# Two decoder layers on one core: the first norm's factor applied behind the GLA products

## The chip, the cores and the metric

The kernel runs on one core of a Trainium2 chip. The metric is the device time of one execution in microseconds (us), as the median of several runs. A core has TensorE (PE in the profile; its weight loads are PEld), VectorE (DVE), ScalarE (ACT), GpSimd (POOL) and SyncE (SP), each with a program of its own, and 16 DMA engines that serve the queues of SP, ACT and POOL.

## The reference, cut to what matters

A prompt of 1024 tokens and eight sample tokens go through two layers of width 1024. Layer 0 has a gated linear attention (GLA, four heads), layer 1 a sliding-window softmax attention; each is followed by a feed-forward layer, and every sub-layer is wrapped in two norms:

```python
def rms_norm(x, g):
    y = xf * lax.rsqrt(jnp.mean(xf * xf, axis=-1, keepdims=True) + NORM_EPS)
    return (y * g.astype(jnp.float32)).astype(x.dtype)
...
h = x @ w_in                      # x is rms_norm(input, norm_mix_pre[0]); 3088 columns
q, k, v, r, z = jnp.split(h, ...) # 512, 512, 1024, 1024, 16
log_a = log_sigmoid(z @ w_gate2 + b_gate) / GLA_TAU
o, s_new = gla_recurrence(q, k, v, log_a, s0)
o = rms_norm(o, g_head) * silu(r)
...
hp = hp + rms_norm(mp, norm_mix_post[layer])
```

The norm in front of the GLA multiplies each feature by a gain and each token by one factor 1 / sqrt(mean(x^2) + eps). A product with `w_in` is linear, so a token's factor can be applied to its input or to each of its results.

## The kernel before

The tokens are worked on in two groups: A is prompt blocks 0 to 3 and the eight samples (520 tokens, in chunks of 256 and 264), B is prompt blocks 4 to 7 (512 tokens, one chunk). Activations have features on partitions, as tiles of 128 features by the tokens of a group, eight tiles for 1024 features.

Each product with a weight matrix is made of column tiles of 128 columns. Weights and activations are split into a high and a low part (`xh`, `xl`, `wh`, `wl`), and for each of eight feature tiles three products are added up: high by high (L217), low by high (L219), high by low (L221), 24 for one column tile and one chunk. `prep` fetches a column tile in two halves on SP's queue (three staging buffers `wst`), casts the high part on ScalarE (L204) and subtracts on VectorE (L205). A job is one column tile; its weights are prepared one job ahead. Results lie in three PSUM buffers (`ps_lin`); transposes and small products use five others (`aux`).

Work other than the jobs is background: generators in one queue, advanced by `tick` according to the us of products emitted since. The tile framework then orders each engine's instructions by readiness and program order; `keep_in_program_order` puts an instruction behind the one traced before it on its engine.

The first phase, group A: `load_x` fetches blocks of 128 tokens by 1024 features, tokens on partitions, on SP's queue. For each block `norm` squares and sums (ScalarE, L438), forms the factor in small steps (L441 to L446) and multiplies the block by factor and gain (VectorE, L449; the gain was fetched broadcast to 128 partitions). `turn` transposes the block on TensorE (L459) and splits it (L289, L290). Behind the third to fifth block come the weights of the gate's input z (`prep_z`) and of the first two column tiles of r. Then, chunk by chunk, z (L247), r0 and r1 are multiplied, and from r2 (t = 2) on the jobs run: six more tiles of r, then for each head q, k and two tiles of v. `gla_gate` turns z into decay tiles `eq` and `ek` for a head, one head ahead; `ev_q` and `ev_k` (L585, L589) multiply q and k by them on the way out of PSUM. `gla_inner` is the background work of a head: transposes, states (`Sp`, cleared by GpSimd at L650), sample states stored from GpSimd's queue (L710), norm. B's `load_x` is the first background task, with B's blocks brought in one by one into one buffer.

Later, after the output projections, `norms` adds the residual and normalises for the feed-forward layer. For the first sub-layer the residual is the input itself (`from_input`): for each of eight feature tiles it is fetched again on ACT's queue, turned on TensorE (L364; for A the samples too, L371) and added on VectorE (L366, L372). For later sub-layers (`from_scratch`) it is read from a scratch tensor `xs` in device memory that already has features on partitions, and added without TensorE. `need(nA)` forces A's norm to be complete ahead of its feed-forward layer.

Of the kernel before, what the change touches and what calls it, by code (L numbers as in the profile page):

```python
# [31 lines left out]
# tiles in a hidden block; buffers  # L32
# [6 lines left out]
# jobs of a feed-forward layer ahead of the projections put into it, and after its attention  # L39
# [4 lines left out]
# how thinly the background work is spread: factors for each norm, then the samples' and the prompt's attention  # L44
# [12 lines left out]
# and steps, in us of matrix products  # L57
# [11 lines left out]
def tile_hybrid_gla_swa_decoder(  # L69
# [10 lines left out]
    # two groups of tokens, features on partitions: A = prompt blocks 0..3 and the samples, B = blocks 4..7  # L80
# [37 lines left out]
    def halved(t, n, name):  # L118
        """-0.5 t, for the factor -2 that rstd_gen leaves"""
        o = const.tile([P, n], F32, name=name)  # L120
        nc.vector.tensor_scalar_mul(o, t, -0.5)
        return o

# [5 lines left out]
    def load_params():  # L129
# [11 lines left out]
        nc.vector.tensor_scalar_mul(bq8, bqkv_t[:, 0:8], 0.125)  # L141

# [21 lines left out]
    def after(jobs, gen, scale=1.0):  # L164
        """the jobs, and a task that is added when the last of them has been emitted"""
# [25 lines left out]
    def prep(w, row0, kt, col0, m, dst=None):  # L191
        parts = []
        for hf in range(kt // 4):
            st = wpool.tile([P, 4, P], F32, tag="wst", name="wst", bufs=WS)
            nc.sync.dma_start(
                out=st[:, :, :m],
                in_=w[row0 + hf * 512 : row0 + hf * 512 + 512, col0 : col0 + m].rearrange(
                    "(k p) m -> p k m", p=P))
# [1215 lines left out]
```

## Time and profile before

| | |
|---|---|
| runs before | 2284.96, 2286.06, 2286.59 us; median 2286.06 us |
| profiled execution: span | 2282.3 us; the page gives no other time for it |
| what lies around the span | 2286.06 - 2282.3 = 3.8 us, the median against the span |
| TensorE busy | 2255.3 us, 99% |
| VectorE, ScalarE, GpSimd busy | 1463.2, 1230.0 and 81.7 us (64%, 54%, 4%) |

A busy share counts an engine as busy from the start of an instruction to its modelled end; products overlap in the pipeline, so the distance between starts is the better measure of what one costs. An idle time is put down to what ended it last.

### The profile page before, as it was taken

The numbers are of one execution on the slowest core, as the hardware profiler recorded it, in microseconds if no ns is written. First come the engines' busy times: TensorE is split into PE (matmuls) and PEld (weight loads), VectorE is DVE, ScalarE is ACT, GpSimd is POOL, SyncE is SP. The second block draws the span as 40 slices with busy tenths as digits, with TensorE's granted clock in tenths as the row PEclk, the third lists the DMA queues.
The fourth block names the chain that finished last, engine by engine and source line by source line (L and its number), as shares of the span: only waits on it lengthen the run. The fifth ranks groups of instructions, "written<-read, shape, count | busy, mean of one in ns | idle before, by whom it ended". The sixth has DMA issues, their size and how long they took to land.

```text
span 2282.3 us, 39657 instructions
## 1 busy us (share of the span) xinstructions
PE 2255.3 (99%) x14764; PEld 2053.8 (90%) x14764; DVE 1463.2 (64%) x3186; ACT 1230.0 (54%) x2614; POOL 81.7 (4%) x121
## 2 busy tenths in 40 slices
PE   7999999999999999999999999999999999999998
PEld 6998889989999998998888989989999898888887
DVE  6587665676644457566887477658888478444445
ACT  6655544465434446545766456537766456434435
POOL 3010000100000000120000000020000000000000
PEclk9999999999999999999999999999999999999999
DMA  6443322445333335333222354432222353533332
GB/s 169 128 132 92 105 78 77 126 138 155 93 93 93 90 92 172 97 110 93 79 86 77 103 157 131 131 111 77 75 75 78 93 163 110 171 105 97 93 97 83
DMA packets 413634, 246.75 MB, mean 108 GB/s; under 512 B 17817, under 2 KB 400889, under 8 KB 412641
## 3 DMA queue, kind: packets, MB, share of 16 engines
q1 hardware_dynamic: 385344, 196.85, 30.0%
q10 hardware_dynamic: 24000, 25.58, 3.8%
q0 software_dynamic: 4096, 21.79, 2.8%
q8 instruction: 116, 1.90, 0.4%
q14 instruction: 78, 0.63, 0.1%
HBM read 220.67 MB, written 24.25 MB: 107 GB/s over the span
## 4 chain that ended last, share of the span: by engine, by line
PE 95%; DVE 2%; DMA 1%; ACT 1%; issue 0%; POOL 0%; ACTq 0%; DVEq 0%; POOLq 0%
PE psl L219 29%; PE psl L217 29%; PE psl L221 29%; PE psc L978 1%; PE ppt L1007 1%; PE po L1018 1%; PE po L1019 1%; PE pP L657 1%; PE pO L684 0%; PE pO L682 0%; PE pxi L364 0%; PE pvt L629 0%; PE patt L633 0%; DMA cm<-const_cmask_dram 0%; DVE nxn L334 0%
## 5 line engine op out<-in xcount | busy, mean ns | idle before, releaser
L217 PE MATMUL psl<-xh,wh 128*128 128x512 f32 (+2 forms) x2784 | 890.8, 320 | 0.7 <-ACT sr L511 0.3
L221 PE MATMUL psl<-xh,wl 128*128 128x512 f32 (+2 forms) x2784 | 886.0, 318 | 1.8 <-DVE xss L445 1.7
L219 PE MATMUL psl<-xl,wh 128*128 128x512 f32 (+2 forms) x2784 | 886.6, 319 | 0.0
L204 ACT CAST wh<-wst 128x512 fp32r<-128x512 f32 x712 | 440.9, 620 | 717.1 <-PE psl L219 629.7
L205 DVE TENSOR_TENSOR wl<-wst,wh 128x512 fp32r<-128x512 f32 x712 | 497.5, 700 | 347.2 <-ACT wh L204 310.9
L221 PEld LDWEIGHTS psl<-xh,wl 128*128 128x128 f32 x2784 | 523.3, 188 | 39.1 <-DVE wl L205 2.4
L217 PEld LDWEIGHTS psl<-xh,wh 128*128 128x128 f32 x2784 | 524.1, 188 | 37.6 <-ACT sr L511 0.6
L219 PEld LDWEIGHTS psl<-xl,wh 128*128 128x128 f32 x2784 | 523.9, 188 | 35.8
L221 PE MATMUL psl<-hh,wl 128*128 128x256 f32 (+2 forms) x1536 | 487.3, 317 | 0.0
L217 PE MATMUL psl<-hh,wh 128*128 128x256 f32 (+1 forms) x1504 | 479.6, 319 | 0.0
L219 PE MATMUL psl<-hl,wh 128*128 128x256 f32 (+1 forms) x1504 | 479.2, 319 | 0.0
L221 PEld LDWEIGHTS psl<-hh,wl 128*128 128x128 f32 x1536 | 288.9, 188 | 20.5
L217 PEld LDWEIGHTS psl<-hh,wh 128*128 128x128 f32 x1504 | 283.0, 188 | 20.8 <-ACT hh L289 0.3
L219 PEld LDWEIGHTS psl<-hl,wh 128*128 128x128 f32 x1504 | 282.7, 188 | 20.7 <-DVE hl L290 0.3
L793 DVE TENSOR_TENSOR yf<-yf,psl 128x256 f32<-128x256 f32 (+1 forms) x344 | 172.4, 502 | 151.7 <-PE psl L221 150.2
L290 DVE TENSOR_TENSOR hl<-rl,hh 128x256 fp32r<-128x256 f32 (+1 forms) x192 | 98.8, 515 | 144.5 <-ACT hh L289 144.4
L780 ACT ACTIVATE rl<-psl 128x256 f32<-128x256 f32 (+1 forms) x192 | 87.1, 454 | 63.1 <-PE psl L221 57.5
L781 ACT ACTIVATE rl<-rl 128x256 f32<-128x256 f32 (+1 forms) x192 | 94.5, 492 | 4.6
L289 ACT CAST hh<-rl 128x256 fp32r<-128x256 f32 (+1 forms) x192 | 92.3, 481 | 4.7
L305 DVE TENSOR_TENSOR nacc<-nacc,nsq 128x520 f32<-128x520 f32 (+1 forms) x99 | 68.6, 693 | 17.3 <-ACT nsq L304 15.0
L992 ACT ACTIVATE pb<-pb,mx 128x256 f32<-128x256 f32 (+1 forms) x128 | 62.2, 487 | 5.7 <-DVE mx L990 4.7
L984 DVE CUSTOM_DVE_ANT_0 pb<-psc,smask 128x256 f32<-128x256 f32 (+1 forms) x128 | 47.8, 401 | 1.2 <-PE psc L978 1.1
(332 smaller groups left out, 2011.8 us busy)
## 6 DMA issues: line engine op xcount, KB each, us to landing
wst<-in_ffn_w_up_dram SPq DMA_DIRECT2D x256, 256.0 KB
wst<-in_ffn_w_down_dram SPq DMA_DIRECT2D x256, 256.0 KB
wst<-in_gla_w_in_dram SPq DMA_DIRECT2D x96, 256.0 KB
wst<-in_swa_w_qkv_dram SPq DMA_DIRECT2D x48, 256.0 KB
wst<-in_gla_w_out_dram SPq DMA_DIRECT2D x32, 256.0 KB
wst<-in_swa_w_out_dram SPq DMA_DIRECT2D x32, 256.0 KB
nx<-xs ACTq DMA_DIRECT2D x24, 260.0 KB
xs<-y POOLq DMA_DIRECT2D x2, 2080.0 KB, 7.9
```

Source lines behind the costliest of these rows:

```text
L204: nc.scalar.copy(out=wh[:, :, :m], in_=st[:, :, :m])
L205: nc.vector.tensor_tensor(out=wl[:, :, :m], in0=st[:, :, :m], in1=r(wh[:, :, :m]), op=ALU.subtract)
L217: nc.tensor.matmul(o, lhsT=wh[:, k % 4, :m], rhs=xh[:, k, c0:c0 + n], start=(k == 0), stop=False)
L219: nc.tensor.matmul(o, lhsT=wh[:, k % 4, :m], rhs=xl[:, k, c0:c0 + n], start=False, stop=False)
L221: nc.tensor.matmul(o, lhsT=wl[:, k % 4, :m], rhs=xh[:, k, c0:c0 + n], start=False, stop=(k == kt - 1))
L289: nc.scalar.copy(out=h, in_=src)
L290: nc.vector.tensor_tensor(out=l, in0=src, in1=r(h), op=ALU.subtract)
L305: nc.vector.tensor_tensor(out=acc, in0=acc, in1=sq, op=ALU.add)
L780: nc.scalar.activation(out=rl, in_=ps, func=AF.Relu)
L781: nc.scalar.activation(out=rl, in_=rl, func=AF.Square)
L793: nc.vector.tensor_tensor(out=o, in0=o, in1=ps, op=ALU.add)
L992: nc.scalar.activation(out=pb[:, i, k0:], in_=pb[:, i, k0:], func=AF.Exp, bias=mx[:, i:i + 1], accum_out=st[:, 2 + i:3 + i])
```

## The change

Group A's input is no longer normalised before it is turned. `load_a` works on two blocks at a time: it transposes the raw blocks, two feature tiles at a time (`turn_pair`: four transposes into one PSUM tile), multiplies by the gain only (now one column `g1` with features on partitions, made by transposing a small tile `g8`), and splits. The squares and the factors are taken beside it. The factors reach all partitions as `rsA` by a product of ones with a diagonal tile `dg`. The raw transposed input is copied from PSUM and written to `xs` from ACT's queue, eight transfers of 256 KB, so A's first residual is read by `from_scratch`; `from_input` stays for B.

The factor then goes to the results: z and r are multiplied by `rsA` as they leave PSUM, on VectorE (r left by ScalarE before); `eq` and `ek` of each head are multiplied by `rsA` on GpSimd; v's turned tiles are scaled on ScalarE, in four instructions in place of two, and the samples' v on VectorE.

The order of the first phase changes too: blocks 0 and 1, both halves of r0's weights, r1's weights (into a free half of scratch), z's weights (one transfer in place of two), blocks 2 and 3 and the samples are all fetched on SP without waiting for a buffer. The weights of r0 are prepared between the turned pairs; r1's low parts are subtracted on GpSimd. Chunk 0 is multiplied as r0, r1, z, with the second pair's turning put in between, then chunk 1. `load_gate` moves behind these products, and its two instructions, the small `halved` ones and one other are pinned in program order. B's input is loaded two blocks at a time by `load_b` with more steps: scaled on ScalarE, turned by `turn_pair`. A's raw blocks now lie in the buffer of B's low parts. The rest of the diff removes comments.

```diff
+    g8 = const.tile([KT, P], F32, name="g8")
+    nc.scalar.dma_start(out=g8, in_=n_mix_pre[0].rearrange("(k p) -> k p", p=P))
+    g1 = const.tile([P, KT], F32, name="g1")
+    pg = aux([P, KT], "pg")
+    nc.tensor.transpose(pg, g8, ident[:KT, :KT])
+    nc.vector.tensor_copy(out=g1, in_=pg)
...
+    def prep(w, row0, kt, col0, m, dst=None, pin=False, sts=None, between=(), eng=None):
...
+                st = sts[hf]
             if dst is None:
                 wh = wpool.tile([P, 4, P], F32R, tag="wh", name="wh", bufs=WB)
...
-            nc.scalar.copy(out=wh[:, :, :m], in_=st[:, :, :m])
-            nc.vector.tensor_tensor(out=wl[:, :, :m], in0=st[:, :, :m], in1=r(wh[:, :, :m]),
-                                    op=ALU.subtract)
+            pinned(nc.scalar.copy(out=wh[:, :, :m], in_=st[:, :, :m]), pin)
+            pinned((eng or nc.vector).tensor_tensor(out=wl[:, :, :m], in0=st[:, :, :m], in1=r(wh[:, :, :m]),
+                                                    op=ALU.subtract), pin)
             parts.append((wh, wl))
+            if hf < len(between):
+                between[hf]()
...
-            if g.ns:
-                xm = npool.tile([NS, P], F32, tag="xsm", name="xsm", bufs=1)
-                nc.scalar.dma_start(out=xm, in_=x_sample[:, 0, k * P:(k + 1) * P])
-                ps = aux([P, NS], "pxs")
-                nc.tensor.transpose(ps, xm, ident[:NS, :NS])
-                nc.vector.tensor_tensor(out=y[:, k, TB:TB + NS], in0=y[:, k, TB:TB + NS], in1=ps, op=ALU.add)
...
-    gbc, xtk = scr[:, 0:D], scr[:, 3 * D:4 * D]
+    rsA, xsm, zt = scr[:, 0:NMAX], scr[:, NMAX:NMAX + 128], scr[:, NMAX + 128:NMAX + 392]
+    xtk = [scr[:, D:2 * D], scr[:, 3 * D:4 * D]]
+    A.rt = const.tile([P, 5], F32, name="rtA")
...
+    def turn_pair(k, tiles, h, l, c0, pin):
+        pt = aux([P, 2, 256], "xT")
+        for i in range(2):
+            for q in range(2):
+                nc.tensor.transpose(pt[:, q, i * P:(i + 1) * P], tiles[i][:, (k + q) * P:(k + q + 1) * P], ident)
+        for q in range(2):
+            hk, lk, g_ = h[:, k + q, c0:c0 + 256], l[:, k + q, c0:c0 + 256], g1[:, k + q:k + q + 1]
+            pinned(nc.scalar.activation(out=hk, in_=pt[:, q, :], func=AF.Copy, scale=g_), pin)
+            pinned(nc.vector.scalar_tensor_tensor(out=lk, in0=pt[:, q, :], scalar=g_, in1=r(hk),
+                                                  op0=ALU.mult, op1=ALU.subtract), pin)
+        return pt
...
+    def load_a(h, l, pair, tiles):
+        c0 = pair * 256
+        ns = NS if pair == 1 else 0
+        n = 3 if ns else 2
+        ss = gp.tile([P, 9], F32, tag="xss", name="xss", bufs=4)
...
+        prs = aux([P, 512], "prs")
+        squares(ss, 0, tiles[0])
+        raw = []
+        for k in range(0, KT, 2):
+            raw.append(turn_pair(k, tiles, h, l, c0, True))
+            yield
+        pinned(squares(ss, 1, tiles[1]))
+        if ns:
+            pinned(squares(ss, 2, tiles[2], NS))
+        y = A.rt[:, 2 * pair:2 * pair + n]
+        factors(ss, n, y)
...
+        N = 256 + ns
+        dg = nt(N, "dg")
+        for i in range(2):
+            nc.vector.tensor_scalar_mul(dg[:, i * P:(i + 1) * P], ident, y[:, i:i + 1])
+        nc.tensor.matmul(prs[:, :256], lhsT=ones, rhs=dg[:, :256], start=True, stop=True)
...
+        nc.scalar.copy(out=rsA[:, c0:c0 + N], in_=prs[:, :N])
+        for k, pt in zip(range(0, KT, 2), raw):
+            t = gp.tile([P, NMAX], F32, tag="qd" if k < 4 else "ki", name="xr", bufs=2)
+            t = t[:, :512].rearrange("p (k t) -> p k t", t=256)
+            pinned(nc.scalar.copy(out=t, in_=pt))
+            nc.scalar.dma_start(out=xs[0][:, k:k + 2, c0:c0 + 256], in_=t)
...
+    def load_b():
+        h, l = new_xn(B)
+        xB.append((h, l))
+        for pair in range(2):
+            ss = gp.tile([P, 9], F32, tag="xss", name="xss", bufs=4)
+            for i in range(2):
+                fetch(B, 2 * pair + i, xtk[i])
+            yield YD
+            for i in range(2):
+                squares(ss, i, xtk[i])
+            y = const.tile([P, 2], F32, name=f"rtB{pair}")
+            factors(ss, 2, y)
+            yield YD
+            for i in range(2):
+                nc.scalar.activation(out=xtk[i], in_=xtk[i], func=AF.Copy, scale=y[:, i:i + 1])
+                yield YN
+            for k in range(0, KT, 2):
+                turn_pair(k, xtk, h, l, pair * 256, False)
+                yield YN
...
         def ev_z(ps, c0, n):
             z = g.z3[:, c0:c0 + n]
+            if g.rs is not None:
+                t = zt[:2 * RANK, :n]
+                nc.vector.tensor_tensor(out=t, in0=ps, in1=g.rs[:2 * RANK, c0:c0 + n], op=ALU.mult)
+                ps = t
...
-            return lambda ps, c0, n: nc.scalar.copy(out=g.sr[:, t, c0:c0 + n], in_=ps)
+            def f(ps, c0, n):
+                o = g.sr[:, t, c0:c0 + n]
+                if g.rs is None:
+                    nc.scalar.copy(out=o, in_=ps)
+                else:
+                    pinned(nc.vector.tensor_tensor(out=o, in0=ps, in1=g.rs[:, c0:c0 + n], op=ALU.mult),
+                           t == 0 and c0 == 0)
+            return f
...
             t0 = 2
             pre_z()
+            tiles = [x0[:, n * D:(n + 1) * D] for n in range(4)] + [xtk[1]]
+            h, l = new_xn(A)
+            early.append((h, l))
+            for n in range(2):
+                fetch(A, n, tiles[n])
+            first = load_a(h, l, 0, tiles[:2])
+            w0 = prep(w_in[0], 0, KT, 2048, P, pin=True, between=[lambda: (next(first), next(first))])
+            sts = [xtk[0][:, i * 512:i * 512 + 512].rearrange("p (k m) -> p k m", m=P) for i in range(2)]
+            for st, row in zip(sts, (0, 512)):
+                fetch_w(st, w_in[0], row, 2048 + P, P)
+            st = fetch_z(w_in[0], 3072)
+            for n in range(2, 4):
+                fetch(A, n, tiles[n])
+            nc.sync.dma_start(out=tiles[4][:NS], in_=x_sample[:, 0, :])
+            next(first)
+            next(first)
+            w1 = prep(w_in[0], 0, KT, 2048 + P, P, pin=True, sts=sts, eng=nc.gpsimd)
+            for _ in first:
+                pass
+            wz = prep_z(st, True)
+            second = load_a(h, l, 1, tiles[2:])
             g.sr = new_big(g, "sr")
-            for c in g.chunks:
-                mms_z(wz[0], x, [c], ev_z)
-                for t in range(t0):
-                    mms(wz[1 + t], KT, P, x, [c], ev_r(t))
+            for i, c in enumerate(g.chunks):
+                mms(w0, KT, P, x, [c], ev_r(0))
+                if i == 0:
+                    next(second)
+                mms(w1, KT, P, x, [c], ev_r(1))
+                if i == 0:
+                    for _ in second:
+                        pass
+                mms_z(wz, x, [c], ev_z)
+            load_gate()
             load_params()
             tick(14.0)
...
+        if g.rs is not None:
+            for t in (eq, ek):
+                nc.gpsimd.tensor_tensor(out=t[:, :N], in0=t[:, :N], in1=g.rs[:, :N], op=ALU.mult)
         g.gate[hd] = (eq, ek, av)
...
+            if g.rs is None:
+                nc.scalar.copy(out=vtok[:, 2 * b2:2 * b2 + 2, :].rearrange("p n (t d) -> p (n t) d", d=P), in_=pt)
+            else:
+                for n in range(2):
+                    nc.scalar.activation(out=vtok[:, 2 * b2 + n, :].rearrange("p (t d) -> p t d", d=P),
+                                         in_=pt[:, 2 * n:2 * n + 2, :], func=AF.Copy,
+                                         scale=g.rt[:, 2 * b2 + n:2 * b2 + n + 1])
...
-            nc.vector.tensor_copy(out=vst, in_=pt[:, 1:3, :].rearrange("p t d -> p (t d)"))
+            nc.vector.tensor_scalar_mul(vst, pt[:, 1:3, :].rearrange("p t d -> p (t d)"), g.rt[:NS, 4:5])
...
-    x0 = new_big(A, "x0").rearrange("p k n -> p (k n)")
...
-    need(tA)
-    load_gate()
-    tB = add(load_x(B, xB, [xtk] * 4), SLB)
-    for g, box, ts in ((A, xA, [tA]), (B, xB, [tB])):
+    x0 = apool.tile([P, KT, B.N], F32, tag="xl1", name="x0").rearrange("p k n -> p (k n)")
+    A.rs, B.rs = rsA, None
+    tB = add(load_b(), SLB)
+    for g, box, ts in ((A, xA, []), (B, xB, [tB])):
...
     jobs, nA = after(out_proj(A, w_out[0], lambda: oA[-1], A.inner + [tSA]),
-                     norms(A, gains["mpost", 0], gains["fpre", 0], xA, from_input), S0)
+                     norms(A, gains["mpost", 0], gains["fpre", 0], xA), S0)
```

## Rows read from the trace of the kernel before

**Rows 1.** The page, busy time of each engine in us, its share, its instructions.

```profile
PE 2255.3 (99%) x14764; PEld 2053.8 (90%) x14764; DVE 1463.2 (64%) x3186; ACT 1230.0 (54%) x2614; POOL 81.7 (4%) x121
```

**Rows 2.** Waits of PE, whole span: total us, how often, longest us.

```profile
PE xT L459 <- DVE x L449: 8.8, 1, 8.8
PE psz L247 <- DVE wz L235: 1.8, 1, 1.8
...
PE psl L221 <- DVE xss L445: 1.7, 2, 1.5
...
PE pxi L364 <- DMA nxi<-in_x_prompt_dram: 0.7, 1, 0.7
```

**Rows 3.** Windows: start and end, length, busy us (instructions) by engine, clock, DMA.

```profile
core 0: us, PE busy (x) PEld busy (x) DVE busy (x) ACT busy (x) POOL busy (x), PEclk, DMA share, GB/s
0.00:8.80 8.80, 0.00 (x0) 0.01 (x1) 1.67 (x7) 4.58 (x10) 7.23 (x22) 1.00 0.79 258
8.80:14.50 5.70, 3.89 (x16) 3.12 (x16) 5.28 (x15) 4.29 (x11) 5.21 (x7) 1.00 0.88 174
14.50:39.20 24.70, 20.82 (x160) 18.17 (x161) 16.68 (x48) 12.50 (x33) 5.55 (x11) 1.00 0.60 143
39.20:207.00 167.80, 166.21 (x1371) 162.59 (x1370) 115.28 (x257) 100.81 (x202) 10.55 (x21) 1.00 0.45 129
440.00:468.00 28.00, 27.23 (x133) 20.77 (x132) 22.95 (x46) 12.88 (x24) 1.95 (x5) 1.00 0.58 172
```

**Rows 4.** Timeline of PE: start us, us, engine, line, operation, how many.

```profile
39.53 0.29 PE L217 MATMUL psl<-xh,wh 128*128 128x256 f32 x1
...
42.38 0.28 PE L217 MATMUL psl<-xh,wh 128*128 128x264 f32 x1
...
45.27 0.28 PE L217 MATMUL psl<-xh,wh 128*128 128x256 f32 x1
...
51.03 1.04 PE L459 MATMUL xT<-ident,scr 128*128 128x128 f32 x8
```

**Rows 5.** Timeline of ACT in the first phase; in brackets idle before, and releaser.

```profile
4.58 1.06 ACT L438 ACTIVATE xsq<-x 128x1024 f32<-128x1024 f32 x1 [2.25 <-DMA x<-in_x_prompt_dram]
...
6.29 1.04 ACT L438 ACTIVATE xsq<-x 128x1024 f32<-128x1024 f32 x1
...
25.82 0.37 ACT L511 COPY sr<-psl 128x256 f32<-128x256 f32 x1
...
34.86 0.60 ACT L204 CAST wh<-wst 128x512 fp32r<-128x512 f32 x1
```

**Rows 6.** The chain that ended last, four full fp32 products of 256 columns.

```profile
105.09 1.73 PE pP L657 x8
```

**Rows 7.** Timeline of PE in A's first residual, one feature tile.

```profile
449.65 0.40 PE L217 MATMUL psl<-xh,wh 128*128 128x512 f32 x1
449.98 0.22 PE L371 MATMUL pxs<-ident,xsm 8*128 8x8 f32 x1
450.14 0.66 PE L364 MATMUL pxi<-ident,nxi 128*128 128x128 f32 x4
450.55 0.48 PE L219 MATMUL psl<-xl,wh 128*128 128x512 f32 x1
```

**Rows 8.** Timeline of DVE, the end of A's norm ahead of its feed-forward layer.

```profile
486.44 1.30 DVE L290 TENSOR_TENSOR xl<-nxn,xh 128x520 fp32r<-128x520 f32 x2
```

**Rows 9.** Groups of POOL by form (busy us, mean ns); timeline of DVE beside one.

```profile
L867 POOL TENSOR_TENSOR qsw<-qsw,sin 128x520 f32<-128x520 f32 x10 | 17.1, 1711 | 88.4 <-DMA qsw<-kr 53.5 <-DMA qsw<-q 31.2 <-DVE wl L205 3.8
...
971.88 0.69 DVE L205 TENSOR_TENSOR wl<-wst,wh 128x512 fp32r<-128x512 f32 x1 [2.12 <-ACT wh L204]
...
973.33 1.79 DVE L205 TENSOR_TENSOR wl<-wst,wh 128x512 fp32r<-128x512 f32 x1
```

**Rows 10.** Timelines of ACT, DVE and POOL, decay tiles and q of one head.

```profile
131.82 0.62 ACT L567 ACTIVATE ek<-ta 128x512 f32<-128x512 f32 x1
...
141.76 0.40 DVE L585 SCALAR_TENSOR_TENSOR qd<-psl,eq 128x256 f32<-128x256 f32 x1
...
155.63 0.31 POOL L650 MEMSET Sp<- 128x256 f32 x1 [28.96 <-PE pO L684]
```

More of the change, by code (lines that the diff above doesn't have):

```diff
@@ L189, in tile_hybrid_gla_swa_decoder, with pinned, fetch_w @@
     pending = []
-    def prep(w, row0, kt, col0, m, dst=None):
-        parts = []
[L193 to L198, printed above, removed]
+    def pinned(ins, pin=True):
+        return tc.keep_in_program_order(ins) if pin else ins
+    def fetch_w(st, w, row, col0, m):
+        nc.sync.dma_start(out=st[:, :, :m],
+                          in_=w[row:row + 512, col0:col0 + m].rearrange("(k p) m -> p k m", p=P))
+    def prep(w, row0, kt, col0, m, dst=None, pin=False, sts=None, between=(), eng=None):
+        parts = []
+        n = kt // 4
+        if sts is None and between:
+            sts = [wpool.tile([P, 4, P], F32, tag="wst", name="wst", bufs=WS) for _ in range(n)]
+            for hf, st in enumerate(sts):
+                fetch_w(st, w, row0 + hf * 512, col0, m)
+        for hf in range(n):
+            if sts is None:
+                st = wpool.tile([P, 4, P], F32, tag="wst", name="wst", bufs=WS)
+                fetch_w(st, w, row0 + hf * 512, col0, m)
+            else:
+                st = sts[hf]
             if dst is None:
@@ L223, in mms, with fetch_z, prep_z @@
             evac(o, c0, n)
[L225 to L235 removed]
+    def fetch_z(w, col0):
+        st = wpool.tile([P, 4, P], F32, tag="wst", name="wst", bufs=WS)
+        st = st.rearrange("p a b -> p (a b)")[:, :KT * RANK].rearrange("p (k m) -> p k m", m=RANK)
+        nc.sync.dma_start(out=st, in_=w[:, col0:col0 + RANK].rearrange("(k p) m -> p k m", p=P))
+        return st
+    def prep_z(st, pin=False):
+        wz = gp.tile([P, KT, 2 * RANK], F32R, tag="wz", name="wz", bufs=1)
+        wh, wl = wz[:, :, :RANK], wz[:, :, RANK:]
+        pinned(nc.scalar.copy(out=wh, in_=st), pin)
+        pinned(nc.vector.tensor_tensor(out=wl, in0=st, in1=r(wh), op=ALU.subtract), pin)
         return wz
@@ new lines, in squares @@
+    def squares(ss, i, tile, rows=P):
+        jk = gp.tile([P, D], F32, tag="Sp", name="xsq", bufs=1)
+        return nc.scalar.activation(out=jk[:rows], in_=tile[:rows], func=AF.Square, accum_out=ss[:rows, i:i + 1])
+    def turn_pair(k, tiles, h, l, c0, pin):
[9 more added lines that the diff above has]
+        return pt
@@ new lines, in fetch @@
+    def fetch(g, n, tile):
+        row = (g.b0 + n) * P
+        nc.sync.dma_start(out=tile, in_=x_prompt[0, row:row + P, :])
+    def load_a(h, l, pair, tiles):
[4 more added lines that the diff above has]
+        if ns:
+            nc.gpsimd.memset(ss, 1.0)
+            pt = aux([P, KT, NS], "xTs")
+            for k in range(KT):
+                nc.tensor.transpose(pt[:, k, :], tiles[2][:NS, k * P:(k + 1) * P], ident[:NS, :NS])
+            t = xsm[:, 0:KT * NS].rearrange("p (k s) -> p k s", s=NS)
+            u = xsm[:, KT * NS:2 * KT * NS].rearrange("p (k s) -> p k s", s=NS)
+            pinned(nc.vector.tensor_copy(out=u, in_=pt))
+            nc.gpsimd.dma_start(out=xs[0][:, :, TB:TB + NS], in_=u)
+            nc.vector.tensor_tensor(out=t, in0=u, in1=g1.unsqueeze(2).to_broadcast([P, KT, NS]), op=ALU.mult)
+            split(h[:, :, TB:TB + NS], l[:, :, TB:TB + NS], t)
+        prs = aux([P, 512], "prs")
[5 more added lines that the diff above has]
+        pinned(squares(ss, 1, tiles[1]))
+        if ns:
+            pinned(squares(ss, 2, tiles[2], NS))
[6 more added lines that the diff above has]
+        nc.tensor.matmul(prs[:, :256], lhsT=ones, rhs=dg[:, :256], start=True, stop=True)
+        if ns:
+            nc.vector.tensor_scalar_mul(dg[:NS, 256:N], ident[:NS, :NS], y[:NS, 2:3])
+            nc.tensor.matmul(prs[:, 256:N], lhsT=ones[:NS], rhs=dg[:NS, 256:N], start=True, stop=True)
+        nc.scalar.copy(out=rsA[:, c0:c0 + N], in_=prs[:, :N])
[4 more added lines that the diff above has]
+            nc.scalar.dma_start(out=xs[0][:, k:k + 2, c0:c0 + 256], in_=t)
@@ L484, in gla_part1 @@
+    def gla_part1(g, x, needs, early=None):
         cell = {}
```

99 lines of the change are left out of this document (18 added, 81 removed).

## The prediction

> **What bounds the kernel now.** I read the page's busy times first: TensorE is busy 99% of the span [rows 1], so time can only come from its idle stretches or from work that it no longer does. The list of TensorE's waits comes next [rows 2]. The reader is to see that nearly all of it lies in the first phase: 8.8 us until the first transposition, which waits for a normalised block, then 1.8 us for z's weights and 1.7 us in the first column tiles. Outside that phase the change touches one wait, 0.7 us for a transfer of the residual. The windows [rows 3] size the first phase: TensorE does nothing up to 8.8 us, is busy 3.9 of the next 5.7 us and 20.8 of the 24.7 us up to 39.2 us, and then 99%. The job of r2, the first that is not part of the old preamble, starts at 39.53 us [rows 4]. The granted clock is 1.00 throughout, so no part of the loss is the clock's. I take two questions from this: when does r2 start after the change, and what happens to the transposes of A's first residual.
>
> **The first phase: TensorE's share.** What must be done before r2 costs TensorE, by distances between starts: 24 products of 256 columns take 42.38 - 39.53 = 2.85 us, 24 of 264 columns 45.27 - 42.38 = 2.89 us [rows 4], so r0 and r1 over both chunks are 11.5 us. That is 0.12 us a product, so z's 32 are 3.8 us. Eight transposes take 1.04 us [rows 4], so 32 are 4.2 us. The eight small ones of the samples are 450.14 - 449.98 = 0.16 us each [rows 7], 1.3 us. New are the two products that spread the factor: full fp32 products of 256 columns, four of which take 1.73 us [rows 6], so 0.9 us for two. The sum is 21.7 us. All but the 0.9 us is done before, too, with one block of B's transposes (1.04 us) besides; so TensorE's work hardly changes, and the gain can only be idle time.
>
> **The first phase: what feeds it.** The first raw block is there at 4.58 us, where ScalarE stops waiting for it; the second was used at 6.29 us without a wait [rows 5], so it landed between the two; I take 5.3 us. The transposes need both blocks. r0's two weight halves, 0.52 MB, are next on SP's queue; at the 258 GB/s of the first 8.8 us [rows 3] that is 2.0 us, so the first half is there at about 6.3 us. From here ScalarE is the narrowest engine. Its prices: 0.60 us for a weight cast, 0.37 us for 256 columns out of PSUM, 1.06 us for the squares of a block [rows 5], about 0.2 more to read the sum. In program order: cast, four high parts, cast, four high parts end at 6.3 + 0.6 + 1.5 + 0.6 + 1.5 = 10.5 us; r1's two casts 11.7; squares of block 1 13.0; the factor through small steps on two engines, the diagonal tile, the product and its copy about 15.7 (estimate: before, block 0's factor takes from the end of its squares at 5.7 us to TensorE's first start at 8.8 us); four raw copies of 512 columns at 0.6 us 18.1; z's cast 18.5. Chunk 0 of r0 follows ScalarE and ends near 11; r1 waits for GpSimd's two subtractions, at 1.71 us as its nearest row has it [rows 9], so up to about 14.5, and ends near 16; z cannot start before 18.5. TensorE is thus idle some 4 us here. The second pair's eight high parts (3.0 us) follow at 18.5 to 21.5, and TensorE then has z and all of chunk 1, 10.2 us, which ends at 28.7 if nothing is in the way. ScalarE still has squares, copies of z, raw copies and r2's casts, about 9 us, after 21.5: it would be through at 31. I take 30 for r2's start. The bounds: dense from 5.3 us it is 27.0; if ScalarE, the eight writes to `xs` or the pinned small instructions hold r2 up as far as r2's distance before allows, I put it at 36.
>
> The gain is 39.5 - 30 = 9.5 us, less the 1.04 us of B's block and 0.3 us of the gate's first products, which before lay ahead of r2 and now behind it: **8.2 us**, from 2.2 to 11.2.
>
> The small parameter loads on GpSimd's queue and the pinned `halved` operations behind them need no data of the first phase; they cost nothing as long as the loads have landed by about 30 us. Before, VectorE ran all of these without a wait. If that cover goes, VectorE waits with r2's low part behind it, and that is inside the bound of 36.
>
> **A's first residual.** One feature tile: a product starts at 449.65, then the sample's transpose, four transposes, and the next product at 450.55; less a product's own 0.23 us (512 columns, eight such steps in a row there) that is 0.67 us [rows 7]. Eight tiles are 5.4 us, with the 0.7 us of waiting [rows 2] 6.1 us that TensorE no longer spends. But this is worth only as much as A's norm moves with it: the norm's last low part ends at 487.7 us [rows 8], just when the feed-forward layer, already begun, needs it. VectorE is busy 22.95 of 28 us there [rows 3], so it can close up by 5.05 us, and by 1.3 us more because eight additions for the samples (0.16 us each) go. In place of L366 there is an addition of the same size, and one transfer from `xs` in place of two from the input. So up to 6.1 us can be had; I take **5.0**, from 0 (the norm's chain does not close up, and TensorE waits for it instead) to 6.1.
>
> **The rest.** B is turned in eight groups of four transposes, 0.67 - 0.16 = 0.5 us each, in place of four groups of eight at 1.04 us: +0.2 us within jobs. v's copies become four of 0.37 us in place of two of 0.6: 0.3 us of ScalarE for each head, hidden, since it is busy 100.8 of 167.8 us in that stage [rows 3]. r's results move to VectorE, busy 115.3 of 167.8: twelve more of about 0.4 us after r2, hidden by the three accumulators. GpSimd's eight products for the decay tiles cost 1.71 us each [rows 9]; the next head's q needs the tile about 9.3 us after it is made (132.4 to 141.8) [rows 10], 3.4 us are used of that: zero. If that cover is gone, see the second rival.
>
> **Sum.** -8.2 - 5.0 + 0.2 = -13.0 us. Span 2282.3 - 13.0 = 2269.3; with the 3.8 us by which the median lies above the span, **2273.1 us**.
>
> **The rivals.** (1) *The residual's gain is given back*: A's norm is bound by VectorE and its small steps, TensorE waits at the feed-forward layer; 2286.1 - 8.2 + 0.2 = 2278.1. For it: the norm ends just in time [rows 8]. Against it: VectorE's idle time there, most of which it spent waiting for these very transposes. (2) *Slower, by GpSimd's order*: the products for the decay tiles stand in one stream with the clearing of `Sp`, which waits 29 us for the previous head's last use of it [rows 10], and with the stores of sample states. Queued behind it, head 2's tiles come at 155.9 + 3.4 = 159.3, 17.5 us after q's result wants them at 141.8. TensorE can go on for two more accumulators, 2.85 + 2.89 us; 11.8 us are lost. One head so delayed eats the gain (2284.9, no change), two decide (2296.7), three give 2308.5. Against it: the tiles are ready 23 us before that clearing can run, so an order by readiness puts them first. GpSimd's own slowness adds to it: VectorE's subtraction beside such a product took 1.79 us in place of 0.69 [rows 9], so each of the two engines holds the other up. The Trainium skill (SBUF — State Buffer, Who interferes with whom) says that a VectorE instruction with two SBUF inputs and a GpSimd one that reads SBUF exclude each other for the whole instruction. By that rule ten such products would cost VectorE up to 17 us, by the row 11 us; the trace agrees in kind, and either way VectorE has 52 us free in the stage. (3) *The first phase stays fed too slowly*: r2 at 36 us gives 2286.1 - 2.2 - 4.8 = 2279.1. For it: ScalarE's list is long, and eight transfers are issued from its queue. (4) *More than forecast*: r2 at 27 and the whole 6.1 us: 2286.1 - 11.2 - 6.1 + 0.2 = 2269.0.
>
> **How the numbers follow.** Forecast 0.60 (2270 to 2277), rival 1 0.12, rival 3 0.10, rival 4 0.12, rival 2 0.06. The range has 2 in 10 left out: most of rival 2, and the edges of 3 and 4: 2267 to 2280.5. A measurement of this kernel tells 0.2%, 4.6 us, from no change. Faster by more: the forecast, 1, 4 and most of 3, 0.86. Within: what is left of 3 and one delayed head, 0.09. Slower: two or more delayed heads, 0.05.
>
> **What would show it.** In the profile after: TensorE's first transposes near 5.5 us and r2's first product near 30 us; a gap of some 4 us before z's first products; no `pxi` for A's tiles, and the norm's last low part some 5 us earlier relative to the jobs around it; no wait of TensorE on `qd` or `ki`. The prediction is wrong if TensorE waits for A's norm at the feed-forward layer, if GpSimd's products start behind an `Sp` clearing, or if r2 starts after 34 us.

## The result, and the profile after

The changed kernel takes 2298.19 us (median of four runs, 2297.56 to 2298.92) against 2286.07 us: ratio 1.0059, 95% interval 1.0047 to 1.0071. It is 12.1 us slower, where 13 us faster was forecast. The profiled execution's span is 2295.7 us, 13.4 more than before. TensorE's busy time hardly changed against [rows 1]; what it lost, it stood still or ran at the lower clock. The page, busy us of each engine:

```profile
PE 2260.9 (98%) x14731; PEld 2057.5 (90%) x14731; DVE 1463.6 (64%) x3181; ACT 1240.7 (54%) x2624; POOL 96.7 (4%) x133
```

TensorE's waits after the change, total us, how often, longest:

```profile
PE prs L506 <- DVE dg L505: 5.0, 2, 4.7
PE pnorm L336 <- ACT nah L311: 4.8, 1, 4.8
PE pg L129 <- DMA g<-in_norm_mix_pre_dram: 4.7, 1, 4.7
PE pso L796 <- ACT sh L311: 3.2, 1, 3.2
...
PE psl L239 <- DVE sr L574: 0.9, 1, 0.9
```

The start's 8.8 us of [rows 2] have shrunk to 4.7, as meant, and three new waits of 3 to 5 us stand beside it. The windows place them: those of [rows 3], and three short ones around the waits (columns as there):

```profile
0.00:8.80 8.80, 3.74 (x17) 3.35 (x18) 1.25 (x3) 3.96 (x7) 7.93 (x25) 1.00 0.86 246
8.80:14.50 5.70, 5.02 (x24) 3.67 (x22) 3.77 (x8) 3.76 (x10) 0.65 (x1) 1.00 1.14 270
14.50:39.20 24.70, 17.69 (x132) 14.80 (x132) 11.40 (x33) 15.98 (x37) 12.90 (x18) 0.96 0.71 188
36.00:48.00 12.00, 7.24 (x31) 6.49 (x32) 3.78 (x14) 6.76 (x16) 0.00 (x0) 0.57 0.56 181
39.20:207.00 167.80, 162.24 (x1288) 157.82 (x1289) 113.93 (x258) 99.69 (x194) 19.10 (x24) 0.97 0.41 117
120.00:140.00 20.00, 16.17 (x121) 15.26 (x119) 16.54 (x37) 9.42 (x21) 5.97 (x9) 0.91 0.30 94
440.00:468.00 28.00, 27.86 (x146) 23.75 (x145) 24.77 (x44) 14.29 (x28) 7.41 (x15) 1.00 0.64 185
474.00:484.00 10.00, 5.22 (x17) 4.10 (x16) 4.35 (x9) 4.86 (x10) 0.00 (x0) 0.68 0.59 159
```

The same three short windows before the change:

```profile
36.00:48.00 12.00, 10.69 (x89) 10.27 (x88) 10.26 (x27) 8.62 (x22) 0.00 (x0) 1.00 0.45 133
120.00:140.00 20.00, 19.89 (x164) 18.80 (x164) 16.89 (x43) 13.48 (x33) 2.65 (x8) 1.00 0.50 145
474.00:484.00 10.00, 10.00 (x46) 8.29 (x45) 9.93 (x19) 7.05 (x13) 0.00 (x0) 1.00 0.30 89
```

TensorE's first phase is ahead up to 14.5 us and then falls behind. In each of the short windows it stands still for 3.8 to 4.8 us in all, and the granted clock, 1.00 in these stretches before, drops toward 0.50, that is from 2.4 to 1.2 GHz, and is still there when products flow again.

**Place 1, r2.** Timeline of TensorE, then of ScalarE, after the change (start us, us, engine, line, operation; in brackets idle before, and releaser):

```profile
34.83 0.28 PE L269 MATMUL psz<-xh,wz 128*32 128x264 f32 x1
...
39.83 1.22 PE L506 MATMUL prs<-dg,ones 128*128 128x256 f32 x2 [4.72 <-DVE dg L505]
...
42.51 0.58 PE L239 MATMUL psl<-xh,wh 128*128 128x256 f32 x1 [0.94 <-DVE sr L574]
```

```profile
32.35 1.05 ACT L453 ACTIVATE xsq<-x 128x1024 f32<-128x1024 f32 x1
...
36.60 0.62 ACT L224 CAST wh<-wst 128x512 fp32r<-128x512 f32 x1 [1.35 <-DMA wst<-in_gla_w_in_dram]
37.12 0.20 ACT L444 ACTIVATE rtA<-xss 128x3 f32<-128x3 f32 x1
37.23 1.04 ACT L453 ACTIVATE xsq<-scr 128x1024 f32<-128x1024 f32 x1
...
41.61 0.38 ACT L510 COPY scr<-prs 128x264 f32<-128x264 f32 x1 [3.15 <-PE prs L509]
```

Chunk 1's products end near 35 us, with r0, r1 and z in the three accumulators. Each leaves PSUM through a product with `rsA`, whose second half does not exist yet: the pair's squares are kept behind all its turned pairs (32.35 us), and the factor's small steps queue on ScalarE behind a cast that waits for its weights and behind a square of group B. `rsA` is there at 42.0 us, and r2 starts at 42.51, against 39.53 in [rows 4].

**Place 2, head 1's q.** VectorE's timeline, before and after:

```profile
108.94 0.41 DVE L585 SCALAR_TENSOR_TENSOR qd<-psl,eq 128x256 f32<-128x256 f32 x1
```

```profile
128.28 0.76 DVE L680 SCALAR_TENSOR_TENSOR qd<-psl,eq 128x256 f32<-128x256 f32 x2
...
129.28 2.93 DVE L312 TENSOR_TENSOR sl<-s,sh 128x256 fp32r<-128x256 f32 x3
```

q leaves PSUM 19 us later, for both chunks together, and behind it three `sl`, 0.42 us each when undisturbed, take 2.93, beside GpSimd's products. From 118.0 us the three accumulators hold q's two chunks and k's first, so TensorE has no place for another column tile; it works through head 0's small products and then stands 3.25 us until ScalarE has cast head 0's states (`sh`, in the list of waits). Its next product of a column tile starts at 128.92 us, behind q.

**Place 3, the last output projection.** Timelines of GpSimd, SP and ScalarE after the change:

```profile
468.61 0.54 POOL L394 DMA_DIRECT2D xs<-y  x1 [15.90 <-DMA wst<-in_gla_w_out_dram]
...
469.35 2.97 SPq L203 DMA_DIRECT2D wst<-in_gla_w_out_dram  x3
...
477.40 0.62 ACT L224 CAST wh<-wst 128x512 fp32r<-128x512 f32 x1 [5.63 <-DMA wst<-in_gla_w_out_dram]
```

`xs<-y` is the write of A's finished first residual, 2080 KB. Before, it was issued at 467.83 us, 10.6 us later relative to A's last copy, when all weights of this projection had been requested. Now weights fetched 0.7 us behind it arrive 8 us later, `nah` stands behind their cast on ScalarE, and TensorE waits for both.

Below, each run's time and its ratio to the kernel before, which was timed anew beside each group of runs (2284.0 to 2286.1 us), and from its profiled execution four starts: r2's first product, q of head 1 leaving PSUM, and the last copy of A's and of B's output projection.

| run | us | ratio, 95% | r2 | q | A | B |
|---|---|---|---|---|---|---|
| before | 2286.07 | | 39.53 | 108.94 | 434.17 | 486.49 |
| after | 2298.19 | 1.0059, 1.0047 to 1.0071 | 42.51 | 128.28 | 445.52 | 499.08 |
| e1_split_store | 2294.62 | 1.0038, 1.0023 to 1.0053 | 42.62 | 127.56 | 444.86 | 497.05 |
| e1b_late_store | 2297.00 | 1.0058, 1.0042 to 1.0075 | 42.86 | 127.88 | 445.19 | 497.93 |
| e8_act_store | 2291.63 | 1.0031, 1.0019 to 1.0043 | 42.79 | 128.95 | 446.94 | 492.93 |
| e2_input_residual | 2299.38 | 1.0060, 1.0045 to 1.0075 | 39.91 | 131.90 | 448.05 | 502.85 |
| e3_early_factor | 2298.60 | 1.0058, 1.0042 to 1.0075 | 40.45 | 129.48 | 444.50 | 498.49 |
| e4_slb | 2300.79 | 1.0067, 1.0052 to 1.0082 | 42.18 | 128.21 | 446.85 | 502.48 |
| e5_eq_dve | 2294.57 | 1.0043, 1.0028 to 1.0058 | 43.29 | 109.90 | 440.49 | 495.43 |
| e6_pin_gate | 2295.56 | 1.0047, 1.0032 to 1.0062 | 41.94 | 126.98 | 442.95 | 496.60 |
| e9_before_pool | 2301.27 | 1.0074, 1.0061 to 1.0088 | 38.73 | 130.69 | 450.08 | 504.77 |
| e10_order | 2297.19 | 1.0052, 1.0039 to 1.0066 | 41.66 | 122.23 | 442.27 | 495.59 |
| c1_late_early_eq | 2288.64 | 1.0016, 1.0007 to 1.0026 | 40.57 | 104.58 | 435.23 | 488.67 |
| c2_early_eq_actstore | 2282.30 | 0.9992, 0.9983 to 1.0001 | 39.98 | 106.32 | 436.76 | 484.88 |
| c3_order_all | 2285.98 | 1.0004, 0.9995 to 1.0013 | 39.87 | 118.91 | 438.86 | 486.20 |
| c4_residual_back | 2290.13 | 1.0024, 1.0015 to 1.0033 | 40.07 | 105.47 | 435.78 | 490.37 |
| c5_mid_squares | 2282.81 | 0.9993, 0.9984 to 1.0002 | 41.34 | 105.68 | 436.23 | 483.85 |
| c6_fresh_buffers | 2280.71 | 0.9982, 0.9973 to 0.9991 | 40.44 | 104.49 | 434.53 | 481.51 |

### The profile page after: what moved, and what is told of

Same layout as the page of the kernel before. It is cut to its first block, busy times and chain, and to the rows that moved or that the text cites. A ratio compares the mean times of both kernels' runs of the same rounds, so it can differ in the third digit from the quotient of the medians.

```text
span 2295.7 us, 39598 instructions
## 1 busy us (share of the span) xinstructions
PE 2260.9 (98%) x14731; PEld 2057.5 (90%) x14731; DVE 1463.6 (64%) x3181; ACT 1240.7 (54%) x2624; POOL 96.7 (4%) x133
## 4 chain that ended last, share of the span: by engine, by line
PE 54%; DVE 1%; DMA 0%; ACT 0%; issue 0%; DVEq 0%; ACTq 0%
PE psl L239 16%; PE psl L241 16%; PE psl L243 16%; PE psc L1079 1%; PE ppt L1108 1%; PE po L1119 1%; PE po L1120 1%; DMA wst<-in_ffn_w_down_dram 0%; PE pfin L1267 0%; PE pyt L1330 0%; PE pxt L1312 0%; PE scT L1192 0%; PE pOs L1245 0%; DVE wl L225 0%; DVE xtail L1379 0%
```

## The experiments

Theory: three separate losses, one in each place. All kernels but e9 start from the changed one.

### The write of the residual: e1, e1b, e8

```diff
# e1: one write for each feature tile, inside post_norm
             residual(k)
+            nc.gpsimd.dma_start(out=xs[0][:, k, :], in_=y[:, k, :])
# e1b and e8: behind the second norm; e1b on GpSimd's queue, e8 on ScalarE's, kept in program order
-        nc.gpsimd.dma_start(out=xs[g.i], in_=y)
...
         yield from pre_norm(y, g, gpre, h, l)
+        nc.gpsimd.dma_start(out=xs[g.i], in_=y)            # e1b
+        pinned(nc.scalar.dma_start(out=xs[g.i], in_=y))    # e8
```

> Edit: the 2 MB write of A's first residual to `xs` leaves as eight writes of one feature tile, each behind that tile's addition, in place of one behind the last. Theory (the freed residual loop brings this one write ahead of the output projection's last weight fetches, which then wait for it): ScalarE's weight cast no longer waits 5.6 us near 477 us, TensorE's wait of 4.8 us for `nah` and the granted clock of 0.50 between 478 and 484 us go, and the time falls by 6 to 8 us to 2290 to 2292. Rival (the norm's own chain on VectorE and ScalarE is what TensorE waits for, and the write is innocent): the wait for `nah` stays and the time stays within 1 us of 2298.2.

> Edit: the 2 MB write of A's first residual is issued behind A's second norm, in place of ahead of it. Theory (whatever else moves data while the last output projection's weights are due delays them; the first split only spread the write over the same stretch): no wait of TensorE over 1 us between 440 and 500 us, granted clock 1.00 there, 2298.2 less 6 to 8 us: 2290 to 2292. Rival (the eight reads of the residual from `xs` are themselves what the weights wait for): 2294 to 2296, as with the split write.

> Edit: the 2 MB write of A's first residual goes to ScalarE's queue and is kept there behind the last high part of A's second norm. (In the run before this one the write, on GpSimd's queue, was only written later in the program and still issued at 467.6 us, so it moved nothing.) Theory (that write is what the last output projection's weight fetches wait for): the wait of 5.6 us of ScalarE for a weight near 477 us and TensorE's 4.8 us for `nah` go; 2298 less 5 to 8 us: 2290 to 2293. Rival (the reads of the residual, or the norm's own chain): within 1.5 us of 2298.

e1 gained 4.8 us by the ratios (1.0059 to 1.0038), less than the 6 to 8 expected: the wait for `nah` went, but the pieces were issued from 458.3 to 470.5 us and still shared that stretch with the weights. e1b moved nothing, since the framework issued the write at 467.57 us as soon as `y` was ready; its expectation fell for that reason and says nothing on the theory. e8 moved it to 491.04 us: the ratio falls from 1.0059 to 1.0031, 6.4 us. Windows of e8, and ScalarE's cast of the same weights:

```profile
474.00:484.00 10.00, 10.00 (x47) 8.13 (x46) 9.20 (x19) 7.06 (x15) 0.00 (x0) 1.00 0.48 140
```

```profile
475.12 0.62 ACT L224 CAST wh<-wst 128x512 fp32r<-128x512 f32 x1 [0.98 <-DMA wst<-in_gla_w_out_dram]
...
491.04 0.33 ACTq L401 DMA_DIRECT2D xs<-y  x1
```

TensorE is busy all the 10 us, at full clock. Place 3 is the write's.

### The residual itself: e2, c4

e2 reads A's first residual from the input again and drops the raw copies; c4 does the first alone, on c2 (below), where the write is out of the way.

```diff
-                     norms(A, gains["mpost", 0], gains["fpre", 0], xA), S0)
+                     norms(A, gains["mpost", 0], gains["fpre", 0], xA, from_input), S0)
# e2 too
-            pinned(nc.scalar.copy(out=t, in_=pt))
-            nc.scalar.dma_start(out=xs[0][:, k:k + 2, c0:c0 + 256], in_=t)
```

> Edit: A's first residual is read from the input and turned again, as before the change; the raw copies in the first phase and their eight writes go. All else is as after the change. Theory (the residual's gain was eaten by the stall near 477 us, and the raw copies cost the first phase a little): 2294 to 2298, with TensorE no longer waiting for `nah`. Rival (the residual's gain of 5.0 us is there, as predicted, and the loss lies elsewhere): 2303.

> The kernel of early squares, VectorE's products and late write (2282.3 us), with one thing undone: A's first residual is read from the input and turned on TensorE; the raw copies stay, so the first phase is the same. Theory (the prediction's price of the residual, 5.0 us, holds once the write is out of the way): 2286 to 2288.5. Rival (A's norm closes up no further, the transposes were free): 2281 to 2284.

e2 came out between the two expectations, and 2.6 us earlier at r2 but later at A: it mixes effects and decides nothing. c4 is clean: 1.0024 against 0.9992, 7.3 us, more than the 5.0 forecast, and B's last copy 5.5 us later. TensorE's wait for the turned input is part of that (0.7 us in [rows 2]):

```profile
PE pxi L386 <- DMA nxi<-in_x_prompt_dram: 2.3, 2, 1.3
```

### The second factor: e3

```diff
# second pair only: squares, factors, dg, prs and the copy to rsA, and then
+            yield from turned()      # the four turned pairs
```

> Edit: for the second pair of blocks and the samples, squares, factor, its spreading product and the copy to `rsA` come ahead of the pair's turning in place of behind it. Theory (chunk 1's three accumulators could not be emptied until its factor existed, so TensorE stood still from 35 to 42 us and then ran at a granted clock of 0.50): r2's first product at 35 to 37 us in place of 42.5, granted clock 1.00 there, 2298.2 less 7 to 9 us: 2289 to 2291. Rival (ScalarE's list as a whole is too long, so that what moves ahead delays the turning by as much): r2 not before 40 us, 2295 to 2298.

The clock stays at 1.00 and r2 comes at 40.45 us, where the rival had it, since ScalarE's squares now delay chunk 1. By q of head 0 the run is 4.8 us ahead (82.86 against 87.70 us for its second chunk). Yet the time is the same: q of head 1 leaves at 129.48. What place 1 gained was lost in place 2:

```profile
36.00:48.00 12.00, 12.00 (x102) 11.69 (x102) 7.86 (x25) 9.73 (x18) 0.00 (x0) 1.00 0.65 188
120.00:140.00 20.00, 14.30 (x94) 12.18 (x93) 14.04 (x32) 7.48 (x18) 5.92 (x9) 0.74 0.42 132
```

### Around head 1: e4, e5, e6, e9, e10

```diff
-SLB = 1.5
+SLB = 1.25                                                    # e4
-                nc.gpsimd.tensor_tensor(out=t[:, :N], in0=t[:, :N], in1=g.rs[:, :N], op=ALU.mult)
+                nc.vector.tensor_tensor(out=t[:, :N], in0=t[:, :N], in1=g.rs[:, :N], op=ALU.mult)   # e5
# e6: gates of heads 2 and 3 kept in program order
+            pinned(nc.scalar.activation(out=ta[:, c0:c0 + n], in_=pt[:, :n], func=AF.Abs, bias=b), late)
# e9: the kernel before, with the products added, by ones
+                nc.gpsimd.tensor_tensor(out=v, in0=v, in1=ones.unsqueeze(1).to_broadcast([P, 4, P]), op=ALU.mult)
# e10: e6, and head 1's ev_q and head 0's first state addition kept in program order
```

> Edit: one number; B's load is charged 1.25 in place of 1.5 for each step, so that its larger number of steps takes about as much of the products' time as before the change. Theory (head 0's inner work started 14 us later than before and met the next gate's on VectorE, busy without a pause from 118.6 to 133 us): TensorE's 3.3 us of waiting for `sh` near 127 us and the clock of 0.50 to 0.86 behind it go, 4 to 6 us less: 2292 to 2294. Rival (GpSimd's products for the decay tiles hold VectorE up, wherever they fall): the time stays within 1.5 us of 2298.2.

> Edit: the products that put the factor on the decay tiles `eq` and `ek` run on VectorE in place of GpSimd. Theory 1 (GpSimd's products hold VectorE's `sl` up, 2.93 us for three after the change and 4.21 for four with the early factor, against 0.4 each): `sl` is back at 0.42 each, TensorE idles 1.5 to 3 us less between 120 and 135 us: 2294 to 2297. Theory 2 (it is the order of the work in VectorE's and ScalarE's queues there, which has the next gate ahead of head 0's sample states; VectorE is already busy without a pause, and these products add 2 x 0.7 us to it): 2298 to 2300.

> Edit: for the gates of heads 2 and 3 of group A, the first instruction on ScalarE and on VectorE is kept behind the one written before it, so that the gate can't be brought ahead of head 0's sample states. Theory (order of the queues, theory 2): ScalarE's casts `sh` no longer stand behind the gate's two exponentials, TensorE's waits for `sh` near 125 us go, 2298.2 less 3 to 5 us: 2293 to 2295. Rival (GpSimd's products hold VectorE wherever they stand, theory 1): within 1.5 us of 2298.2.

> The kernel before the change, with one thing added: the decay tiles of each of A's heads are multiplied by ones on GpSimd, eight products of 512 columns. Theory (GpSimd's products by themselves cost time, through VectorE's instructions beside them and the wait for the tiles): 2 to 6 us slower than before, TensorE idle beside the heads. Rival (they cost only where B's longer load has pushed head 0's states into the next gate): within 1.5 us of before.

> Edit: the decay tiles' products stay on GpSimd, but VectorE's queue gets the order that it has with them on VectorE: head 1's q leaves PSUM ahead of head 0's states, and the next gate stands behind. Theory 2a (the cost is the order: q's results, ready near 113 us, stand behind some 20 instructions of head 0's states and the next gate until 128.3, while all three accumulators are full): q leaves by 115 us, TensorE's 3.8 us of idle time near 127 us go, 2298 less 4 to 6 us: 2292 to 2294. Theory 1 (VectorE's instructions are held up by GpSimd's products wherever they stand): within 2 us of 2298.

e4 misses: q still leaves at 128.21 us, but from 120 to 140 us TensorE is busy 18.29 us at 1.00; the idle time moves to 150 to 207 us (54.47 us busy of 57, against 56.86 after the change) and the run is slower, so B's longer load alone isn't it. e5 brings q of head 1 back to 109.90 us and A's last copy 5.0 us forward; some of that is lost again in place 3. It can't tell its two theories apart, since it both takes the products off GpSimd and moves q forward in VectorE's queue. e9 is the clearest. The eight products alone make the kernel before 17 us slower, where 2 to 6 were expected and the changed kernel's whole loss is 13.4. The instructions of `sl` from 100 to 140 us, of after, e5 and e9 in that order (duration in ns: least, median, greatest):

```profile
L312 DVE TENSOR_TENSOR sl<-s,sh x4: 412/420/2261, 129.3 to 139.4; 128x256 fp32r<-128x256 f32 x4
```

```profile
L312 DVE TENSOR_TENSOR sl<-s,sh x8: 417/420/426, 134.9 to 139.5; 128x256 fp32r<-128x256 f32 x8
```

```profile
L290 DVE TENSOR_TENSOR sl<-s,sh x8: 395/416/426, 114.2 to 123.2; 128x256 fp32r<-128x256 f32 x8
```

Its windows:

```profile
120.00:140.00 20.00, 13.62 (x67) 11.39 (x68) 13.60 (x36) 7.81 (x18) 4.53 (x9) 0.57 0.30 94
```

In e9 no `sl` is held up, and still TensorE stands for 6.4 of 20 us. What differs is the place of q in VectorE's queue. Counted over the trace, q's first result is VectorE's 149th instruction before the change and its 187th in e9, behind head 0's states and the next gate. VectorE's timeline in e9 up to q, and TensorE's next product of a column tile:

```profile
113.24 0.87 DVE L708 SCALAR_TENSOR_TENSOR s<-s,av,pkv 128x256 f32<-128x256 f32 x2 [1.79 <-PE pkv L705]
...
127.28 1.01 DVE L305 TENSOR_TENSOR nacc<-nacc,nsq 128x520 f32<-128x520 f32 x1 [1.23 <-ACT nsq L304]
128.97 0.70 DVE L290 TENSOR_TENSOR nal<-nacc,nah 128x520 fp32r<-128x520 f32 x1 [0.69 <-ACT nah L289]
130.35 0.42 DVE L317 TENSOR_SCALAR nms<-pnorm 128x256 f32<-128x256 f32 x1 [0.68 <-PE pnorm L315]
130.69 0.76 DVE L589 SCALAR_TENSOR_TENSOR qd<-psl,eq 128x256 f32<-128x256 f32 x2
```

```profile
131.16 0.59 PE L217 MATMUL psl<-xh,wh 128*128 128x264 f32 x1 [0.63 <-DVE qd L589]
```

Head 1's tiles are multiplied by 98.3 us and q's products end by 109.4 us, and yet VectorE takes q at 130.69. Between, it stands still six times, 6.9 us in all, for results that other instructions need. So q is kept back in e9 by its place in the queue, which the framework fixes when the kernel is built, and not by GpSimd's speed at run time. In the changed kernel q stands as late, as VectorE's 174th instruction against the 146th in e5; there, being held up comes on top (2.26 us for one `sl`). e6 gained 2.7 us by the ratios, with intervals that overlap. e10 got q to the 153rd place and only to 122.23 us, and its four runs span 2293.8 to 2300.1 us: inconclusive. How the cost in the changed kernel divides between order and hold-up was not settled, nor why the framework puts q so late.

### Together: c1, c2, c3, c5, c6

c1 is e1b + e3 + e5. c2 takes e8 for the write, and leaves the spreading product behind the turned pairs. c3 is c2 with e10's order and the products on GpSimd. c5 and c6 alter c2's first phase.

```diff
# c5 and c6: the second pair's raw copies in idle buffers
-            t = gp.tile([P, NMAX], F32, tag="qd" if k < 4 else "ki", name="xr", bufs=2)
+            # second pair: halves of the tiles tagged "vtok" and "vT"
# c5: its squares and factor between the second and third turned pair
```

> Three edits together: the late write, the early second factor, and the decay tiles' products on VectorE. If the three losses are separate and each edit cures its own: 2298.2 less 7 (write), less 5 (first phase, which alone was lost again near 125 us), less 3: 2283 to 2286, that is level with the kernel before. If the stretch near 125 us gives back what the first phase gains whatever GpSimd does: 2289 to 2292.

> Three edits together on the kernel after the change: squares and factor of the second pair ahead of its turning, with the spreading product still behind it; the decay tiles' products on VectorE; the late write from ScalarE's queue. If the three losses are separate: 2288.6 (early factor and VectorE's products, measured with a write that did not move) less 5 to 7 us: 2281 to 2284, faster than the kernel before by 1 to 4 us. If the write is innocent: 2288 to 2290.

> The order of the run before it with the early squares and the late write from ScalarE's queue; the products stay on GpSimd. If the order is the whole cause: as with the products on VectorE, 2281 to 2284. If GpSimd's products also hold VectorE up: 2285 to 2289.

> The fastest version so far (early squares, VectorE's products, late write: 2282.3 us) with two edits in the first phase. The second pair's raw copies go to buffers that nothing else uses then, in place of those of the first pair, whose write to `xs` ScalarE waited 3.9 us for near 35 us, with r2's weight casts behind it. And the second pair's squares stand between its turned pairs, no longer ahead of the first factor. If ScalarE's wait is what holds r2: r2's first product some 2 to 4 us earlier than 40.0 us, 2278 to 2281. If the squares' place matters more: 2282 or above.

> The same fastest version with the first of these edits alone (buffers of their own for the second pair's raw copies). If ScalarE's wait for the write holds r2: 2279 to 2281.5. If PE's idle time ahead of 30 us sets r2 anyway: 2281.5 to 2283.

c1's write didn't move (as in e1b), so the first expectation, without its 7 us for the write, is about 2291; it took 2288.6. c2 is 15.3 us better than the changed kernel (1.0059 to 0.9992), level with the one before; alone, its edits gave 0.2 (e3), 3.7 and 6.4. The difference, 5.0 us, is in the main the first phase's gain, which e3 alone lost again in place 2: c2 is 3.6 us ahead of e5 at q of head 1 and still 3.7 at A's last copy. c3 is 2.7 us slower than c2, with q at 118.91 us against 106.32: the pins brought back only part of the order, so this doesn't separate order and hold-up either. c5's ratio is 0.0011 above c6's, with intervals that overlap, and its r2 comes 0.9 us later: its place for the squares gains nothing. c6, where ScalarE no longer waits for the writes, is faster than both kernels, 4.1 us below the one before (2 to 6 by the interval). Its windows:

```profile
36.00:48.00 12.00, 12.00 (x103) 11.70 (x102) 8.54 (x28) 8.71 (x15) 0.00 (x0) 1.00 0.61 176
120.00:140.00 20.00, 20.00 (x170) 19.30 (x169) 15.34 (x41) 10.99 (x25) 3.23 (x5) 1.00 0.58 167
440.00:468.00 28.00, 26.27 (x118) 20.95 (x117) 25.35 (x45) 16.49 (x34) 1.88 (x4) 1.00 0.64 187
474.00:484.00 10.00, 9.61 (x51) 8.11 (x51) 9.28 (x15) 5.15 (x9) 0.00 (x0) 1.00 0.48 186
```

All three places are all but filled. But r2 still starts at 40.44 us, no earlier than before; the forecast 30 was reached by no version.

## Why the prediction was wrong

The forecast was a span 13.0 us shorter; it is 13.4 longer, 26.4 us apart. Four steps account for it.

**"What feeds it", r2 at 30 us (measured 42.51, 12.5 apart).** The first transposes came at 4.85 and 5.92 us, as forecast. Then the list of ScalarE's work was taken as if nothing stood between its items. High and low parts alternate between ScalarE and VectorE, each waiting 0.5 to 0.8 us for the other; the second pair's transposes wait for the raw copies that free `aux`; chunk 1 ended near 35, not 28.7. The step also had no second factor in it: it let r2 follow chunk 1, while from 35 us three accumulators were waiting for `rsA`. Of the 12.5 us, 6.4 are chunk 1's delay and the rest is that wait with the steps behind it. But with the factor early (e3) chunk 1 ends later and r2 comes only 2.1 us sooner, so ScalarE's list as a whole is the larger part. The bound of 36 was put by distances of the old order and bounded nothing. (The step's 10.2 us for z and chunk 1 comes to 9.6 to 10.1 by its own prices, which changes little.)

**"The granted clock is 1.00 throughout, so no part of the loss is the clock's."** True of the kernel before, and wrongly carried to a kernel with new idle stretches. r2's first 24 products ran at 0.50 up to about 47.4 us and took 5.17 us where they take 2.85: 2.3 us.

**GpSimd's products at zero.** The named cover held: head 1's tiles are ready 24 us before q leaves. The cost came by a way that the step didn't look at, VectorE's queue: in the window from 120 to 140 us TensorE is busy 16.17 us at 0.91 where it was busy 19.89 at 1.00, that is 3.7 us of idle time and 1.5 of clock, 5.2 us; e5, without the products on GpSimd, has A's last copy 5.0 us earlier. Rival 2 had the sign and the engine, but not the place: the products never stood behind an `Sp` clearing (`eq` is there at 127.3 us, its product starts at 128.68).

**A's first residual, -5.0 us.** The mechanism was right and the size too low: 7.3 us where nothing is in the way (c4), above the upper end of 6.1, which had 0.7 us for waits on transfers of the input, where c4 shows 2.3. In the changed kernel it turned into +2.05 (13.4 - 11.35 us of delay at A's last copy), 7.05 from the forecast: the residual did run ahead, and its write met the weights; e8, which moves the write, gets 6.4 us back. This is rival 1's sign by another cause; VectorE did not bind.

The sum, 12.5 + 2.3 + 5.2 + 7.05 = 27.05 us, is within 0.7 of the 26.4. The last term was taken as what is left behind A's last copy, so the sum tests the other three. That r's results on VectorE and v's four copies cost nothing, and B's turning 0.2 us, was right as far as the runs show: in c6, with the three places cured, no wait of TensorE names them. The 3.8 us put on top of the span was too much: in the changed kernel's profiled execution the time lies 1.9 us above the span (2297.56 against 2295.7), so the forecast span of 2269.3 stood for some 2271, not 2273.1.

## What to carry to other kernels

When results wait for a factor, count the accumulators: once all hold results that cannot leave, the factor's chain is TensorE's path, however small its instructions. An instruction put on an idle engine is not free because its result is in time; look at where the build then queues those who read it, and run the old kernel with that one instruction added. And work that is freed moves the large transfers behind it: ask what they will meet at the new time, and check with the program's order that an edit moved what it was to move.

## What was not expected of the hardware

- Three gaps of TensorE, of 3.2 to 4.8 us, were each followed by products at a granted clock of 0.50, though it had run at 1.00 up to the gap: 130 to 132 us (behind an idle stretch from 125.1 to 128.3), 42 to 46 us, 480 to 484 us. The low clock cost nearly half of the gap's length again (1.5 us behind 3.2, 2.3 behind 4.7).
- One `sl`, a subtraction of two tiles in SBUF, took 2.26 us beside GpSimd's products, in place of 0.42, and in e3 four took 4.21 in all. The held one ended at 131.54 us, 0.29 behind GpSimd's second product, and in e3 at 126.71, again 0.29 behind: it sat out two products in a row. A `ki`, with one input from PSUM, took its usual 0.41 beside the first product. The Trainium skill (SBUF — State Buffer, Who interferes with whom) has a VectorE instruction with two SBUF inputs contend with a GpSimd one that reads SBUF, on a shared read interface; the rows agree.
- Behind a 2080 KB write from GpSimd's queue, a 256 KB weight fetch issued 0.74 us later on SP's queue was first used 8 us after its issue, 0.9 us after the write had landed (it took 7.9 us).
